# Two more channel tiles of each depthwise convolution without tap matmuls: products on ScalarE, sums on GpSimd

## The chip, the cores and the metric

The kernel runs on one core of one Trainium2 chip. The metric is the device time of one execution in microseconds (us). The kernel before was timed three times, with a median of 2589.94 us (2589.64 to 2590.89). One further execution was profiled; it took 2588.89 us. All points of time below are microseconds from the start of that execution's span.

## The reference, cut to what matters

The program is a four-layer encoder on 512 tokens and 1024 channels in float32. Layers 0 and 3 use the convolution module as their token mixer, so it runs twice. Only that module is touched:

```python
def dwconv(x, w, b):                      # w is (31, 1024): each channel has its own 31 taps
    k, c = w.shape
    y = lax.conv_general_dilated(x, w[:, None, :], window_strides=(1,),
        padding=[(k // 2, k // 2)], dimension_numbers=('NWC', 'WIO', 'NWC'), feature_group_count=c)
    return y + b

def conv_module(h, w_in, b_in, dw_w, dw_b, ln_g, ln_b, w_out):
    a, gt = jnp.split(h @ w_in + b_in, 2, axis=-1)
    u = a * jax.nn.sigmoid(gt)
    u = dwconv(u, dw_w, dw_b)
    u = layernorm(u, ln_g, ln_b)          # over all 1024 channels of a token
    return jax.nn.silu(u) @ w_out
```

The layer norm needs all channels of a token, so nothing behind it starts before the last channel tile of the convolution is complete.

## The kernel before, in words

The 1024 channels are eight tiles of 128. `conv` works through them in the order `CORDER`. For each tile m, `front(m)` multiplies the input by two weight tiles (value and gate). Each product is three matmuls of 128x512 per 128 input channels (`mm3`, L157 to L159), because a float32 operand is split into a high and a low part: ScalarE casts the high part (L152), VectorE subtracts to get the low part (L153). Then VectorE and ScalarE scale, gate and write the result.

Seven tiles go through TensorE. Their gated result `u` (L407) is spread by four small DMAs on GpSimd's queue (`xf`, L412) and split into `X` (L167, L168). `taps(m, X, half)` loads a prepared matrix of taps per 32 channels (`wraw`, SyncE's queue), splits it into `W` (ScalarE's cast L167, VectorE's subtraction L168) and runs nine pairs of matmuls: L445 (256 columns) and L448 (128 columns). A tile has four such matrices, thus 36 pairs. Two additions on VectorE (L457, L460) bring the sums with the bias into `y`.

One tile, number 6, is made by `direct` on VectorE alone: its gated result is `ud` (L403), and 31 instructions (L421, L423) each multiply a shifted view by one tap and add it to `yd`. Four transposes on TensorE (L428) and a copy on ScalarE (L429) bring it into `y`.

`bn_stats` (L465) reads finished column groups of `y`. Behind the last tap matmul stand 23 matmuls without use (`NWARM`, L470) that fill TensorE's wait for the statistics. Then `norm` starts with transposes (L510), and the output product follows.

The program is built with a scheduler that sets each engine's order from its own model of the times. Within an engine the order is fixed, and an instruction that waits holds everything behind it on that engine. `issue_after` pins an instruction behind another one.

Of the kernel before, what the change touches and what calls it, by code (L numbers as in the profile page):

```python
# [17 lines left out]
P = 128  # L18
# [14 lines left out]
_n = 0  # L33
for _name, _w in (
    ("n1g", 32), ("n2g", 32), ("cbin", 32), ("clg", 16), ("clb", 16), ("qg", 1), ("kg", 1), ("gng", 16), ("logd", 8),
    ("fdw", 4 * 44 * FC), ("fdb", 4 * 44), ("cwd", 2 * CW), ("cbd", 2),
):
    COLS[_name] = _n
    _n += _w
# [20 lines left out]
NRAW = 2  # L60
HPO = 100000
NQZ = 2
BNG = ((0, 8, 8), (8, 14, 12), (14, 15, 15), (15, 16, 16))
NWARM = 23
CD = 6
CORDER = (CD, 0, 1, 2, 3, 4, 5, 7)
CTAPS = (0, 3, 5, 5, 5, 5, 5, 3, 0, 0)


@with_exitstack  # L70
def tile_trunk(
# [17 lines left out]
    def nm(s):  # L89
        uid[0] += 1  # L90
        return f"{s}{uid[0]}"
# [11 lines left out]
    def bank(which):  # L103
        return cur[which].tile([P, T], F32, tag="ps", name=nm("ps"))
# [246 lines left out]

    def conv(j, after):
        with ExitStack() as st:
            stage_pools(st, 9, 4, 4)
            cp = st.enter_context(tc.tile_pool(name=nm("cv"), bufs=1, reuse_waits=RW))
            y = cp.tile([P, SH, D], F32, tag="y", name=nm("y"))
            bias = cp.tile([P, D], F32, tag="bias", name=nm("bias"))
            early = kind == "conv" and j == 0 and bool(first)
            if not early:
                nc.scalar.dma_start(bias, cdb[j])  # L360
            bst = cp.tile([P, SH, len(BNG), 6], F32, tag="bst", name=nm("bst"))
            with ExitStack() as s2:
                up = s2.enter_context(tc.tile_pool(name=nm("cvu"), bufs=1, reuse_waits=RW))
                dp = s2.enter_context(tc.tile_pool(name=nm("cvd"), bufs=2, reuse_waits=RW))
                us = [up.tile([P, SH, QL], F32, tag=f"u{i}", name=nm("u")) for i in range(2)]
                ud = up.tile([P, T + CW - 1], F32, tag="ud", name=nm("ud"))
                yd = up.tile([P, T], F32, tag="yd", name=nm("yd"))
                nc.vector.memset(ud[:, :CW // 2], 0.0)
                nc.vector.memset(ud[:, T + CW // 2:], 0.0)
                for u in us:  # L370
                    nc.vector.memset(u[:, :, :4], 0.0)
                    nc.vector.memset(u[:, :, QL - 4:], 0.0)
# [2 lines left out]
                    nc.vector.tensor_copy(ap, sqacc[:, :1])  # L375

                def front(m):
                    where = psb if early and m == CD else psa
                    pa, pg = bank(where), bank(where)
                    ws = state.pop("first", None) if m == CD else None  # L380
                    if ws:
                        for k in range(KD):
                            s = slice(k * P, (k + 1) * P)
                            for ps, (wh, wl) in zip((pa, pg), ws):
                                mm3(ps, wh[:, s], wl[:, s], xhi[k], xlo[k], k == 0, k == KD - 1)
                        after_squares(bias[:, :1])
                        nc.scalar.dma_start(bias, cdb[j])
                        stats1()
                        stats2()
                    else:  # L390
                        for (ps, c) in ((pg, m + 8), (pa, m)):
                            wh, wl = load_w(cw_in[j, c], D)
                            for k in range(KD):
                                s = slice(k * P, (k + 1) * P)
                                mm3(ps, wh[:, s], wl[:, s], xhi[k], xlo[k], k == 0, k == KD - 1)
                            if m == CD:
                                stats2() if c == m else stats1()
                    ta, tg = t512(), t512()
                    nc.vector.tensor_tensor(tg, pg, rstd_bc, MUL)
                    nc.scalar.activation(tg, tg, AF.Sigmoid, bias=pc("cbin", j * 16 + 8 + m))  # L400
                    nc.vector.tensor_tensor(ta, pa, rstd_bc, MUL)
                    if m == CD:
                        nc.vector.scalar_tensor_tensor(  # L403
                            ud[:, CW // 2:CW // 2 + T], ta, pc("cbin", j * 16 + m), tg, ADD, MUL)
                        return None
                    u = us[m % 2]
                    state["u"] = nc.vector.scalar_tensor_tensor(  # L407
                        u[:, :, 4:4 + P], ta.rearrange("p (q s) -> p s q", s=SH),
                        pc("cbin", j * 16 + m), tg.rearrange("p (q s) -> p s q", s=SH), ADD, MUL)
                    xf = dp.tile([P, 4, QL], F32, tag="xf", name=nm("xf"))  # L410
                    for b in range(4):
                        nc.gpsimd.dma_start(xf[:, b, :], u[32 * b:32 * b + 32])  # L412
                    X = dp.tile([P, 4, 2, QL], F32R, tag="X", name=nm("X"), bufs=3)
                    split(xf, X[:, :, 0, :], X[:, :, 1, :])
                    return X

                def direct(k0, k1):
                    for k in range(k0, k1):
                        w = pc("cwd", j * CW + k)
                        if k == 0:  # L420
                            nc.vector.tensor_scalar(yd, ud[:, :T], w, pc("cbd", j), MUL, ADD)  # L421
                        else:
                            nc.vector.scalar_tensor_tensor(yd, ud[:, k:k + T], w, yd, MUL, ADD)  # L423
                    if k0 < k1 == CW:
                        ps = bank(psb)
                        yr = yd.rearrange("p (q r) -> p r q", r=SH)
                        for r in range(SH):
                            nc.tensor.transpose(ps[:, r * P:(r + 1) * P], yr[:, r], ident)  # L428
                        nc.scalar.copy(y[:, :, CD * P:(CD + 1) * P],  # L429
                                       ps.rearrange("p (r c) -> p r c", r=SH))  # L430

                def taps(m, X, half):
                    ps = bank(psb)
                    for i in range(2):
                        b = half * 2 + i
                        raw = dp.tile([P, NA, P], F32, tag="wraw", name=nm("wraw"), bufs=5)
                        if early and m * 4 + b < 5:
# [3 lines left out]
                        with tc.issue_after(state["u"].ins) if early and m * 4 + b < 5 else ExitStack():  # L441
                            split(raw, W[:, :, 0, :], W[:, :, 1, :])
                        o = ps[:, i * 256:(i + 1) * 256]
                        for a in range(NA):
                            nc.tensor.matmul(o, X[:, b, 0, a:a + P],  # L445
                                             W[:, a].rearrange("p h n -> p (h n)"),
                                             start=a == 0, stop=False)
                            mm = nc.tensor.matmul(o[:, :P], X[:, b, 1, a:a + P], W[:, a, 0, :],  # L448
                                                  start=False, stop=a == NA - 1)
# [3 lines left out]
                    bb = bias[:, c0:c0 + 64].rearrange("p (b c) -> p b c", b=2)  # L453
# [8 lines left out]
                    for n, (a0, a1, at) in enumerate(BNG):  # L462
                        if c1 == at:
                            for r in range(SH):
                                nc.vector.bn_stats(bst[:, r, n, :], y[:, r, a0 * 64:a1 * 64])  # L465
                    if c1 == 16:
                        wp = bank(psa)
                        with tc.issue_after(mm.ins):
# [2 lines left out]
                        with tc.issue_after(state["cast"].ins):  # L471
                            nc.scalar.activation(sm(1), zero, AF.Silu)

                fr, done = {}, 0
                for n in range(10):
                    if n < 8:
                        fr[n] = front(CORDER[n])
                    direct(done, done + CTAPS[n])
                    done += CTAPS[n]
                    if n >= 3:  # L480
                        taps(CORDER[n - 2], fr[n - 2], 1)
                    if 2 <= n <= 8:
                        taps(CORDER[n - 1], fr[n - 1], 0)
            mv = sm(8)
            for r in range(SH):
# [528 lines left out]
    kind, l = seq[0]  # L1014
    first = []
    if kind == "conv":
        for c in (CD, CD + 8):
# [48 lines left out]
def _layout(inp):  # L1066
# [31 lines left out]
    cd = slice(CD * P, (CD + 1) * P)  # L1098
    put("cwd", f["conv_dw_w"][:, :, cd].transpose(2, 0, 1).reshape(P, -1))
    put("cbd", f["conv_dw_b"][:, cd].T)  # L1100
# [74 lines left out]
```

## Time and profile before

| What | us |
|---|---|
| Median of three runs | 2589.94 |
| Profiled execution, its own time | 2588.89 |
| Its span | 2586.8 |
| TensorE busy | 2575.8 |
| VectorE busy | 1664.1 |
| ScalarE busy | 1041.4 |
| GpSimd busy | 229.9 |
| Tap matmuls of the first convolution, from and to | 55.8 to 156.5 |
| First transpose of `norm`, first and second convolution | 162.0 and 2161.7 |

A group row of the profile names line, engine, operation, output and inputs, shape and count, then busy time and mean duration of one in ns, then the idle time of the engine ahead of the group with what ended it. A row of the timeline gives start, duration, engine, line and instruction, and how many equal ones it merges. Matmuls overlap in the timeline, so the pace of a series is read from the distance of two starts, not from a duration. TensorE's granted clock is 1.0 throughout.

### The profile page before, as it was taken

Reading aid. Unit: us, or ns where it says so; the run is one execution under the profiler, and the core shown is the slowest. Engines: PE = TensorE matmul, PEld = TensorE weight load, DVE = VectorE, ACT = ScalarE, POOL = GpSimd, SP = SyncE. Lnnn points to the kernel's source line nnn. Section 1 sums busy time; section 2 is a strip of 40 time slices with the busy share of each in tenths; the row PEclk is TensorE's granted clock in tenths of the full one; section 3 lists DMA queues with packets and bytes.
Section 4 is the critical chain, followed back from the end, with each engine's and each line's share of the span. In section 5 each row is a group of like instructions: output and inputs, shape, how many; then the busy total and the mean of one; then the engine's idle time right before and its main releaser. Section 6 shows DMA issues by size and latency. Waiting matters only on the chain.

```text
span 2586.8 us, 32299 instructions
## 1 busy us (share of the span) xinstructions
PE 2575.8 (100%) x12750; PEld 2138.5 (83%) x12750; DVE 1664.1 (64%) x2688; ACT 1041.4 (40%) x1423; POOL 229.9 (9%) x245
## 2 busy tenths in 40 slices
PE   9999999999999999999999999999999999999999
PEld 7988888889998888888888888888888888788888
DVE  7976777438878777624656566677733877677732
ACT  5454444335555444323333333444422445444421
POOL 0103000003421100000000000100000111100000
PEclk9999999999999999999999999999999999999999
DMA  6724222333332322333222221222233662222232
GB/s 226 230 74 153 98 90 96 90 100 111 97 91 70 99 98 92 92 97 110 74 87 68 88 75 61 101 91 98 89 92 97 215 195 70 93 90 98 89 109 80
DMA packets 78376, 269.86 MB, mean 104 GB/s; under 512 B 9824, under 2 KB 12768, under 8 KB 78224
## 3 DMA queue, kind: packets, MB, share of 16 engines
q1 hardware_dynamic: 73152, 254.49, 30.3%
q0 software_dynamic: 3776, 10.58, 1.5%
q10 hardware_dynamic: 1296, 2.72, 0.3%
q8 instruction: 100, 1.64, 0.3%
q14 instruction: 52, 0.43, 0.1%
HBM read 258.35 MB, written 5.63 MB: 102 GB/s over the span
## 4 chain that ended last, share of the span: by engine, by line
PE 98%; DVE 1%; DMA 0%; ACT 0%; issue 0%; SPq 0%; DVEq 0%
PE ps L157 27%; PE ps L158 27%; PE ps L159 27%; PE ps L445 3%; PE ps L163 3%; PE ps L164 3%; PE ps L162 3%; PE ps L448 1%; PE ps L314 1%; PE ps L315 1%; PE ps L319 1%; PE ps L692 1%; PE ps L470 0%; DMA x<-in_xT 0%; PE ps L510 0%; PE ps L918 0%
## 5 line engine op out<-in xcount | busy, mean ns | idle before, releaser
L152 ACT CAST wh<-wr 128x1024 fp32r<-128x1024 f32 (+1 forms) x410 | 423.0, 1033 | 1077.9 <-PE ps L158 766.3
L158 PE MATMUL ps<-xl,wh 128*128 128x512 f32 x1856 | 735.8, 397 | 0.1
L157 PE MATMUL ps<-xh,wh 128*128 128x512 f32 x1856 | 733.1, 396 | 0.2 <-ACT wh L152 0.2
L159 PE MATMUL ps<-xh,wl 128*128 128x512 f32 x1856 | 731.5, 394 | 0.1
L153 DVE TENSOR_TENSOR wl<-wr,wh 128x1024 fp32r<-128x1024 f32 (+1 forms) x407 | 494.0, 1214 | 327.8 <-ACT wh L152 325.5
L157 PEld LDWEIGHTS ps<-xh,wh 128*128 128x128 f32 x1856 | 348.6, 188 | 86.7 <-ACT wh L152 0.9
L159 PEld LDWEIGHTS ps<-xh,wl 128*128 128x128 f32 x1856 | 348.3, 188 | 84.1 <-DVE wl L153 0.5
L158 PEld LDWEIGHTS ps<-xl,wh 128*128 128x128 f32 x1856 | 348.5, 188 | 82.2 <-DVE xl L216 0.5
L157 PE MATMUL ps<-hh,wh 128*128 128x512 f32 (+1 forms) x726 | 281.8, 388 | 0.5 <-DVE x L344 0.5
L159 PE MATMUL ps<-hh,wl 128*128 128x512 f32 (+1 forms) x726 | 281.8, 388 | 0.0
L158 PE MATMUL ps<-hl,wh 128*128 128x512 f32 (+1 forms) x726 | 281.8, 388 | 0.0
L280 DVE TENSOR_TENSOR t<-ps,rstd_bc 128x512 f32<-128x512 f32 x176 | 121.0, 691 | 158.5 <-PE ps L159 158.5
L234 POOL TENSOR_TENSOR sqacc<-t,sqacc 128x512 f32<-128x512 f32 x49 | 74.5, 1520 | 1262.3 <-ACT t L229 1261.8
L157 PEld LDWEIGHTS ps<-hh,wh 128*128 128x128 f32 x726 | 136.4, 188 | 31.7 <-DVE x L344 0.7
L159 PEld LDWEIGHTS ps<-hh,wl 128*128 128x128 f32 x726 | 136.4, 188 | 30.9
L158 PEld LDWEIGHTS ps<-hl,wh 128*128 128x128 f32 x726 | 136.4, 188 | 30.8
L163 PE MATMUL ps<-wl,xh 128*128 128x256 f32 (+1 forms) x512 | 159.2, 312 | 0.5 <-DVE wl L153 0.5
L164 PE MATMUL ps<-wh,xl 128*128 128x256 f32 (+1 forms) x512 | 159.1, 312 | 0.0
L162 PE MATMUL ps<-wh,xh 128*128 128x256 f32 (+1 forms) x512 | 158.5, 312 | 0.0
L283 ACT ACTIVATE t<-t,par 128x512 f32<-128x512 f32 x176 | 142.5, 814 | 6.7 <-DVE t L280 6.6
L287 DVE SCALAR_TENSOR_TENSOR t<-t,par,t 128x511 f32<-128x511 f32 x176 | 132.2, 751 | 5.6
L285 DVE SCALAR_TENSOR_TENSOR t<-t,par,t 128x511 f32<-128x511 f32 x176 | 131.1, 746 | 0.0
(244 smaller groups left out, 3445.0 us busy)
## 6 DMA issues: line engine op xcount, KB each, us to landing
wr<-in_f_up SPq DMA_DIRECT2D x176, 512.0 KB, 3.3
wraw<-in_cdw SPq DMA_DIRECT2D x56, 576.0 KB, 4.5
wr<-in_f_down SPq DMA_DIRECT2D x64, 448.0 KB, 3.3
wr<-in_f_down SPq DMA_DIRECT2D x32, 512.0 KB, 3.5
wr<-in_cw_in SPq DMA_DIRECT2D x30, 512.0 KB, 4.0
wr<-in_nat_qkv SPq DMA_DIRECT2D x24, 512.0 KB, 3.3
wr<-in_cw_out SPq DMA_DIRECT2D x16, 512.0 KB, 3.6
wr<-in_ret_qk SPq DMA_DIRECT2D x16, 512.0 KB, 3.2
```

The source lines that it names most:

```text
L152: nc.scalar.copy(hi[:, :n], raw[:, :n])
L153: eng.tensor_tensor(lo[:, :n], raw[:, :n], hi[:, :n].bitcast(F32), SUB)
L157: nc.tensor.matmul(o, wh, ah, start=first, stop=False)
L158: nc.tensor.matmul(o, wh, al, start=False, stop=False)
L159: nc.tensor.matmul(o, wl, ah, start=False, stop=last)
L162: nc.tensor.matmul(o, ah, wh, start=first, stop=False)
L163: nc.tensor.matmul(o, ah, wl, start=False, stop=False)
L164: nc.tensor.matmul(o, al, wh, start=False, stop=last)
L280: nc.vector.tensor_tensor(u, ps, rstd_bc, MUL)
L283: nc.scalar.activation(a, u, AF.Identity, bias=pc("fdb", l * 44 + c), scale=pt[:, w + 1:w + 2])
L285: nc.vector.scalar_tensor_tensor(a[:, 1:], u[:, :T - 1], pt[:, w:w + 1], a[:, 1:], MUL, ADD)
L287: nc.vector.scalar_tensor_tensor(a[:, :T - 1], u[:, 1:], pt[:, w + 2:w + 3], a[:, :T - 1], MUL, ADD)
```

## The change: three tiles without tap matmuls

Tiles 1, 6 and 0 now come first and go around the tap matmuls (`CDIR`). Tile 0 gets all 31 taps on VectorE, as tile 6 did before. Tiles 1 and 6 get four taps on VectorE (`CVEC`); each of the other 27 becomes a product on ScalarE into a buffer `pr` (two buffers) and a sum into `yd` on GpSimd. `gather` transposes a finished tile on TensorE, pinned behind a tap matmul, and takes its statistics. `CSTEP` and `CDONE` say behind which front the steps are written down. Five tiles keep their tap matmuls. The temporaries go from nine to seven and the buffers of `wraw` from five to four, since the new tiles need room.

```diff
-BNG = ((0, 8, 8), (8, 14, 12), (14, 15, 15), (15, 16, 16))
+BNG = ((0, 8, ("d", 2)), (8, 12, 12), (12, 14, ("d", 1)), (14, 15, 15), (15, 16, 16))
-CD = 6
-CORDER = (CD, 0, 1, 2, 3, 4, 5, 7)
-CTAPS = (0, 3, 5, 5, 5, 5, 5, 3, 0, 0)
+CORDER = (1, 6, 0, 2, 3, 4, 5, 7)
+CDIR = (1, 6, 0)
+CVEC = (4, 4, 31)
+CSTEP = ((0, 0, 0, 31), (1, 1, 0, 31), (2, 2, 0, 3), (3, 2, 3, 10),
+         (4, 2, 10, 17), (5, 2, 17, 24), (6, 2, 24, 31))
+CDONE = {6: (0,), 7: (2,), 8: (1,)}
...
-            stage_pools(st, 9, 4, 4)
+            stage_pools(st, 7, 4, 4)
...
-                def direct(k0, k1):
+                def direct(i, k0, k1):
+                    ud, yd = uds[i], yds[i]
                     for k in range(k0, k1):
-                        w = pc("cwd", j * CW + k)
+                        w = pc("cwd", (j * 3 + i) * CW + k)
                         if k == 0:
-                            nc.vector.tensor_scalar(yd, ud[:, :T], w, pc("cbd", j), MUL, ADD)
+                            nc.vector.tensor_scalar(yd, ud[:, :T], w, pc("cbd", j * 3 + i), MUL, ADD)
+                        elif k < CVEC[i]:
+                            nc.vector.scalar_tensor_tensor(yd, ud[:, k:k + T], w, yd, MUL, ADD)
                         else:
-                            nc.vector.scalar_tensor_tensor(yd, ud[:, k:k + T], w, yd, MUL, ADD)
-                    if k0 < k1 == CW:
-                        ps = bank(psb)
-                        yr = yd.rearrange("p (q r) -> p r q", r=SH)
+                            pr = up.tile([P, T], F32, tag="pr", name=nm("pr"), bufs=2)
+                            nc.scalar.activation(pr, ud[:, k:k + T], AF.Copy, scale=w)
+                            nc.gpsimd.tensor_tensor(yd, pr, yd, ADD)
+
+                def gather(i):
+                    ps = bank(psb)
+                    yr = yds[i].rearrange("p (q r) -> p r q", r=SH)
+                    with tc.issue_after(state["tap"].ins):
                         for r in range(SH):
                             nc.tensor.transpose(ps[:, r * P:(r + 1) * P], yr[:, r], ident)
...
+                    stats(("d", i))
...
-                        raw = dp.tile([P, NA, P], F32, tag="wraw", name=nm("wraw"), bufs=5)
+                        raw = dp.tile([P, NA, P], F32, tag="wraw", name=nm("wraw"), bufs=4)
...
-                fr, done = {}, 0
+                fr, nd = {}, len(CDIR)
                 for n in range(10):
                     if n < 8:
                         fr[n] = front(CORDER[n])
-                    direct(done, done + CTAPS[n])
-                    done += CTAPS[n]
-                    if n >= 3:
+                    for (at, i, k0, k1) in CSTEP:
+                        if at == n:
+                            direct(i, k0, k1)
+                    if n - 2 >= nd:
                         taps(CORDER[n - 2], fr[n - 2], 1)
-                    if 2 <= n <= 8:
+                    for i in CDONE.get(n, ()):
+                        gather(i)
+                    if nd <= n - 1 < 8:
                         taps(CORDER[n - 1], fr[n - 1], 0)
```

The built order shows the change on the queues that the prediction speaks of. First GpSimd in the second convolution (`xf<-u` are the spreading DMAs, L412 before and L417 now; L433 is the new sum). Before:

```order
L234 TENSOR_TENSOR sqacc<-t_16858,sqacc 128x512
L412 DMA xf_17067<-u_16886 128x1x136 x4
L412 DMA xf_17146<-u_16887 128x1x136 x4
L412 DMA xf_17277<-u_16886 128x1x136 x4
L412 DMA xf_17458<-u_16887 128x1x136 x4
L412 DMA xf_17639<-u_16886 128x1x136 x4
L412 DMA xf_17820<-u_16887 128x1x136 x4
```

Now, from the thirteenth sum on:

```order
L433 TENSOR_TENSOR yd_16869<-pr_17025,yd_16869 128x512
L433 TENSOR_TENSOR yd_16869<-pr_17028,yd_16869 128x512
L417 DMA xf_17362<-u_16864 128x1x136 x4
L433 TENSOR_TENSOR yd_16869<-pr_17031,yd_16869 128x512
L433 TENSOR_TENSOR yd_16869<-pr_17034,yd_16869 128x512
L433 TENSOR_TENSOR yd_16869<-pr_17037,yd_16869 128x512
L433 TENSOR_TENSOR yd_16869<-pr_17040,yd_16869 128x512
L433 TENSOR_TENSOR yd_16869<-pr_17043,yd_16869 128x512
L417 DMA xf_17445<-u_16865 128x1x136 x4
```

GpSimd had nothing but 28 DMAs in a convolution. It now has 54 sums, 27 of one tile and then 27 of the next, with 20 DMAs between them.

Second TensorE near the end of the first convolution's taps, at the transposes of the last direct tile (`yd`). Before, where tile 6 was gathered (L428) ahead of the second half of tile 4's taps:

```order
L159 MATMUL ps_1266<-xh_92,wl_1300 128x512
L428 MATMUL ps_1345<-ident,yd_223 128x128 x4
L445 MATMUL ps_1351<-W_1354,X_973 128x256
L448 MATMUL ps_1351<-W_1354,X_973 128x128
L445 MATMUL ps_1351<-W_1354,X_973 128x256
```

Now, where tile 6 is gathered (L440) ahead of the taps of the last tile, 7 (L463 and L466 are the tap pair):

```order
L463 MATMUL ps_1419<-W_1445,X_1117 128x256
L466 MATMUL ps_1419<-W_1445,X_1117 128x128
L440 MATMUL ps_1473<-ident,yd_226 128x128 x4
L463 MATMUL ps_1483<-W_1486,X_1306 128x256
L466 MATMUL ps_1483<-W_1486,X_1306 128x128
```

The tile that GpSimd finishes last is now gathered ahead of the 36 tap pairs of tile 7 and of the matmuls without use. Until it is complete, TensorE's queue stands there.

Third ScalarE in the first convolution, where the new products (`pr<-ud`, L432) stand among the casts of weights. Before:

```order
L429 COPY y_211<-ps_1345 128x4x128
L167 CAST W_1427<-wraw_1425 128x9x128
L167 CAST W_1454<-wraw_1452 128x9x128
L167 CAST W_1477<-wraw_1475 128x9x128
L167 CAST X_1339<-xf_1334 128x4x136
```

Now:

```order
L171 CAST W_1486<-wraw_1484 128x9x128
L432 ACTIVATE pr_518<-ud_223,par 128x512
L171 CAST W_1509<-wraw_1507 128x9x128
L171 CAST X_1306<-xf_1301 128x4x136
L432 ACTIVATE pr_521<-ud_223,par 128x512
L432 ACTIVATE pr_524<-ud_223,par 128x512
L171 CAST W_1540<-wraw_1538 128x9x128
L432 ACTIVATE pr_527<-ud_223,par 128x512
```

A product waits for the sum that frees its buffer, and the casts that TensorE's taps need stand behind it.

More of the change, by code (lines that the diff above doesn't have):

```diff
@@ L353, in conv @@
         with ExitStack() as st:
[L354 removed]
+            stage_pools(st, 7, 4, 4)
             cp = st.enter_context(tc.tile_pool(name=nm("cv"), bufs=1, reuse_waits=RW))
             y = cp.tile([P, SH, D], F32, tag="y", name=nm("y"))
[L357 removed]
+            bias = cp.tile([P, D - CB], F32, tag="bias", name=nm("bias"))
             early = kind == "conv" and j == 0 and bool(first)
             if not early:
[L360 removed]
+                nc.scalar.dma_start(bias, cdb[j][:, CB:])
             bst = cp.tile([P, SH, len(BNG), 6], F32, tag="bst", name=nm("bst"))
@@ L365, in conv @@
                 us = [up.tile([P, SH, QL], F32, tag=f"u{i}", name=nm("u")) for i in range(2)]
[L366 to L369, printed above, removed]
+                uds = [up.tile([P, T + CW - 1], F32, tag=f"ud{i}", name=nm("ud")) for i in range(3)]
+                yds = [up.tile([P, T], F32, tag=f"yd{i}", name=nm("yd")) for i in range(3)]
+                for ud in uds:
+                    nc.vector.memset(ud[:, :CW // 2], 0.0)
+                    nc.vector.memset(ud[:, T + CW // 2:], 0.0)
                 for u in us:
@@ L377, in front @@
                 def front(m):
-                    where = psb if early and m == CD else psa
+                    where = psb if early and m == CORDER[0] else psa
                     pa, pg = bank(where), bank(where)
-                    ws = state.pop("first", None) if m == CD else None
+                    ws = state.pop("first", None) if m == CORDER[0] else None
                     if ws:
@@ L386, in front @@
                         after_squares(bias[:, :1])
-                        nc.scalar.dma_start(bias, cdb[j])
+                        nc.scalar.dma_start(bias, cdb[j][:, CB:])
                         stats1()
@@ L435, in taps @@
                         b = half * 2 + i
-                        raw = dp.tile([P, NA, P], F32, tag="wraw", name=nm("wraw"), bufs=5)
-                        if early and m * 4 + b < 5:
+                        raw = dp.tile([P, NA, P], F32, tag="wraw", name=nm("wraw"), bufs=4)
+                        if early and CORDER.index(m) * 4 + b < 4 * len(CDIR) + 5:
                             after_squares(raw[:, 0, :1])
@@ L440, in taps @@
                         W = dp.tile([P, NA, 2, P], F32R, tag="W", name=nm("W"), bufs=3)
-                        with tc.issue_after(state["u"].ins) if early and m * 4 + b < 5 else ExitStack():
-                            split(raw, W[:, :, 0, :], W[:, :, 1, :])
+                        split(raw, W[:, :, 0, :], W[:, :, 1, :])
                         o = ps[:, i * 256:(i + 1) * 256]
@@ L461, in taps @@
                     c1 = m * 2 + half + 1
[L462 to L465, printed above, removed]
+                    state["tap"] = mm
+                    stats(c1)
                     if c1 == 16:
@@ L1016, in tile_trunk @@
     if kind == "conv":
-        for c in (CD, CD + 8):
+        for c in (CORDER[0], CORDER[0] + 8):
             first.append((wraw.tile([P, D], F32, tag="wr", name=nm("wr")),
```

26 lines of the change are left out of this document (16 added, 10 removed).

## The prediction

> **What bounds the kernel now.** First the page's busy times and its chain of waits, then the timeline of TensorE in the stage that changes.
>
> ```profile
> PE 2575.8 (100%) x12750; PEld 2138.5 (83%) x12750; DVE 1664.1 (64%) x2688; ACT 1041.4 (40%) x1423; POOL 229.9 (9%) x245
> PE 98%; DVE 1%; DMA 0%; ACT 0%; issue 0%; SPq 0%; DVEq 0%
> ```
>
> TensorE is the chain for 98% of the span, so a matmul that goes is a gain as long as nothing else becomes late. Whether anything does is read from the two stretches of tap matmuls, 55.0 to 156.4 and 2037.0 to 2156.4 (columns: length, then busy us and instructions of each engine, granted clock, DMA share, GB/s):
>
> ```profile
> core 0: us, PE busy (x) PEld busy (x) DVE busy (x) ACT busy (x) POOL busy (x), PEclk, DMA share, GB/s
> 55.00:156.40 101.40, 101.40 (x693) 93.00 (x692) 89.78 (x118) 47.83 (x49) 10.80 (x20) 1.00 0.58 185
> 2037.00:2156.40 119.40, 119.40 (x770) 107.56 (x769) 97.87 (x128) 51.96 (x55) 13.12 (x25) 1.00 0.53 168
> ```
>
> The reader is to see two things. TensorE is never idle and has its full clock, so it does set the end. But VectorE is busy for 89.8 of 101.4 us and 97.9 of 119.4 us: here, unlike in the rest of the program, the second engine is close behind. GpSimd is nearly idle, and it is where the change puts its work.
>
> **The gain on TensorE.** Nine pairs of taps run between the two matmuls of `mm3` below; then the gather of the direct tile and the end of the stage:
>
> ```profile
> 102.14 0.28 PE L445 MATMUL ps<-W,X 128*128 128x256 f32 x1
> 104.17 0.44 PE L158 MATMUL ps<-xl,wh 128*128 128x512 f32 x1
> 135.37 0.63 PE L428 MATMUL ps<-ident,yd 128*128 128x128 f32 x4
> 135.75 0.37 PE L445 MATMUL ps<-W,X 128*128 128x256 f32 x1
> 156.55 5.46 PE L470 MATMUL ps<-xh 128*128 128x512 f32 x23
> 162.04 0.30 PE L510 MATMUL ps<-ident,yn 128*128 128x128 f32 x1
> 2156.16 5.46 PE L470 MATMUL ps<-xh 128*128 128x512 f32 x23
> 2161.66 0.92 PE L510 MATMUL ps<-ident,yn 128*128 128x128 f32 x5
> ```
>
> Nine pairs take 104.17 - 102.14 = 2.03 us, a tile's 36 pairs 8.1 us. Two tiles go per convolution (16.2 us) and two gathers of 0.38 us come: 15.5 us less for TensorE per convolution, 31 us in all. Alone on the path this gives 2588.9 - 31 = 2558 us, the most that the change can bring.
>
> **What ScalarE gets.** 54 products per convolution. No row has one; the nearest 128x512 rows of ScalarE with a scale or bias are these:
>
> ```profile
> L213 ACT ACTIVATE xh<-x,png 128x512 fp32r<-128x512 f32 x64 | 50.7, 798 | 33.3 <-DVE x L523 16.4 <-DVE x L256 12.9 <-DVE x L251 3.6
> L400 ACT ACTIVATE t<-t,par 128x512 f32<-128x512 f32 x16 | 11.5, 723 | 1.9 <-DVE t L399 1.8
> L167 ACT CAST W<-wraw 128x1152 fp32r<-128x1152 f32 x25 | 29.0, 1159 | 34.7 <-PE ps L448 32.5 <-issue 1.3 <-ACT t L400 1.0
> ```
>
> 54 at 0.72 to 0.80 us are 39 to 43 us; eight casts of `W` at 1.16 us (the last row, of the first stretch) go. Net some 32 us on an engine with 47.8 of 101.4 us busy: 80 us, which fits. So ScalarE's time costs nothing by itself; its order may (a rival below).
>
> **What GpSimd gets.** 54 sums per convolution, each reading two tiles from SBUF and writing one, 128x512. The same form exists: `sqacc` (L234). Its rows alone, and then where VectorE splits weights (L153) beside it:
>
> ```profile
> L234 POOL TENSOR_TENSOR sqacc<-t,sqacc 128x512 f32<-128x512 f32 x49 | 74.5, 1520 | 1262.3 <-ACT t L229 1261.8
> 841.40 1.30 POOL L234 TENSOR_TENSOR sqacc<-t,sqacc 128x512 f32<-128x512 f32 x1
> 842.77 1.29 POOL L234 TENSOR_TENSOR sqacc<-t,sqacc 128x512 f32<-128x512 f32 x1
> 846.59 1.29 DVE L153 TENSOR_TENSOR wl<-wr,wh 128x1024 fp32r<-128x1024 f32 x1 [5.40 <-ACT wh L152]
> 846.87 2.16 POOL L234 TENSOR_TENSOR sqacc<-t,sqacc 128x512 f32<-128x512 f32 x1
> 847.80 2.31 DVE L153 TENSOR_TENSOR wl<-wr,wh 128x1024 fp32r<-128x1024 f32 x1
> 849.11 2.15 POOL L234 TENSOR_TENSOR sqacc<-t,sqacc 128x512 f32<-128x512 f32 x1
> 188.29 1.31 POOL L234 TENSOR_TENSOR sqacc<-t,sqacc 128x512 f32<-128x512 f32 x1 [48.33 <-ACT t L229]
> 188.35 1.80 DVE L216 SCALAR_TENSOR_TENSOR xl<-x,png,xh 128x512 fp32r<-128x512 f32 x1
> 1230.64 1.30 POOL L831 TENSOR_TENSOR t<-t,t 128x512 f32<-128x512 f32 x1
> 1231.02 0.68 DVE L827 TENSOR_TENSOR t<-ps,sn 128x512 f32<-128x512 f32 x1
> ```
>
> Alone, sums that follow each other start every 1.37 us. Beside VectorE's splits they start every 2.24 us, and VectorE's split takes 2.31 us where its mean is 1.22 in the groups below. So the two take turns. This concerns VectorE instructions with both tensors in SBUF; the one that reads `ps` (PSUM) runs at its 0.68 us beside a sum. How long a sum shuts VectorE out: the split is 2.31 - 1.22 = 1.09 us longer; the L216 instruction, 1.80 us against the 0.75 us of the same operation on `yd` below, is 1.05 us longer and began 0.06 us behind the sum. I take 1.10 us.
>
> The Trainium skill has a rule for this ("SBUF — State Buffer", section "Who interferes with whom"): a VectorE instruction with two SBUF inputs and a GpSimd instruction that reads SBUF use one shared port, and the later one is blocked until the first has finished. The trace agrees on who blocks whom, but frees the port after about 1.10 of a sum's 1.29 us. By the page's full length the sum below would be 54 x 0.19 = 10 us higher per convolution, 2658 us by estimate.
>
> So I count the turns. VectorE's instructions with two SBUF inputs in both stretches:
>
> ```profile
> L168 DVE TENSOR_TENSOR W<-wraw,W 128x1152 fp32r<-128x1152 f32 x26 | 35.0, 1352 | 2.0 <-ACT W L167 2.0
> L423 DVE SCALAR_TENSOR_TENSOR yd<-ud,par,yd 128x512 f32<-128x512 f32 x24 | 17.9, 746 | 0.1
> L153 DVE TENSOR_TENSOR wl<-wr,wh 128x1024 fp32r<-128x1024 f32 x9 | 10.9, 1221 | 1.6 <-ACT wh L152 1.6
> L407 DVE SCALAR_TENSOR_TENSOR u<-t,par,t 128x512 f32<-128x512 f32 x5 | 5.7, 1146 | 0.1
> L168 DVE TENSOR_TENSOR X<-xf,X 128x544 fp32r<-128x544 f32 x6 | 4.3, 718 | 0.0
> L168 DVE TENSOR_TENSOR W<-wraw,W 128x1152 fp32r<-128x1152 f32 x25 | 33.9, 1357 | 3.2 <-ACT W L167 3.2
> L423 DVE SCALAR_TENSOR_TENSOR yd<-ud,par,yd 128x512 f32<-128x512 f32 x27 | 20.2, 750 | 0.2
> L153 DVE TENSOR_TENSOR wl<-wr,wh 128x1024 fp32r<-128x1024 f32 x12 | 14.6, 1220 | 0.3 <-ACT wh L152 0.3
> ```
>
> In the changed order, behind the fourth VectorE tap of the first direct tile, the first convolution has 17 `W`, 31 `yd`, 9 `wl`, 5 `u` and 5 `X`: 17 x 1.352 + 31 x 0.746 + 9 x 1.221 + 5 x 1.146 + 5 x 0.718 = 66.4 us. The second has 17, 33, 12, 5, 5 and one `ud` (0.75): 72.6 us. With 54 x 1.10 = 59.4 us of sums the port is taken for 125.8 and 132.0 us. VectorE instructions overlap by about 0.09 us (the split at 847.80 starts before the one ahead ends, 846.59 + 1.29), which for 67 and 73 of them takes off 6.0 and 6.6 us; on the other side the port rests whenever both wait. I take half: 122.8 and 128.7 us.
>
> Where it starts: the scale `rstd_bc` must be there.
>
> ```profile
> 35.44 0.59 ACT L247 COPY rstd_bc<-ps 128x512 f32<-128x512 f32 x1 [2.60 <-PE ps L193]
> 2027.64 0.59 ACT L247 COPY rstd_bc<-ps 128x512 f32<-128x512 f32 x1 [2.19 <-PE ps L193]
> L412 POOL DMA_DIRECT2D xf<-u x56 | 30.5, 566 | 236.5 <-DVE u L407 169.6 <-issue 36.4 <-ACT W L167 30.5
> ```
>
> From there to the fourth tap VectorE has some 21 instructions in the first convolution (seven scalings, three gates, two splits, nine taps), about 16 us, and a weight still on its way: first sum near 55 (51 to 57). In the second convolution a dozen, about 9 us: near 2037.
>
> The last sum then ends at 55 + 122.8 = 177.8 and 2037 + 128.7 = 2165.7. TensorE's queue stands at the gather of that tile. Behind it come 0.4 us of transposes, tile 7's 8.1 us of taps and 5.5 us of matmuls without use before `norm`: 14.0 us, giving 191.8 and 2179.7, against 162.0 and 2161.7 now. **That is +29.8 and +18.0, together +48 us.** TensorE's saving is inside it: its taps would be ready near 141 and 2141 and wait. Other stalls of TensorE ahead of that gather cost nothing while it is early by so much.
>
> Bounds from GpSimd's own queue: 20 DMAs at 0.57 us (11.4 us) and 54 sums at 1.37 or 2.24 us are 85 or 132 us. By the first, `norm` starts at 55 + 85.4 + 14.0 = 154.4 (-7.6) in the first convolution, and in the second TensorE sets the end (-15.5): 2566 us. By the second it starts at 55 + 132.4 + 14.0 = 201.4 (+39.4) and 2037 + 132.4 + 14.0 = 2183.4 (+21.7): 2650 us. My 122.8 and 128.7 us correspond to 2.06 and 2.17 us per sum, near the upper row, because VectorE nearly always has such an instruction ready. With p for a sum's price both convolutions together change by 108 p - 181 us, so the zero lies at 1.68 us per sum.
>
> Edits that I cost at nothing: fewer temporaries, four buffers for `wraw` and 24 fewer loads on SyncE's queue in all, covered by TensorE's long wait; if the first lacks cover, a front waits one scaling (0.7 us) each. Tile 0's 31 VectorE taps replace those of tile 6. The DMAs that now stand behind sums on GpSimd delay `X` by up to a sum or two (2 to 4 us), under the same cover. All stages outside the two convolutions keep their order.
>
> The profiled execution is 1.05 us under the median of the runs; with +48 on the median I predict 2638 us.
>
> **Rivals.** *Sums fit in beside VectorE (faster).* If GpSimd keeps its 1.37 us, because the turns are rare, the time is the 2566 us above. For it speaks that most of the 49 `sqacc` rows are nearer to 1.3 than to 2.2 (mean 1.52). Against it: those ran where VectorE had gaps, and here VectorE is busy for 89%. It decides below 1.68 us. Chance 0.08.
>
> *ScalarE's order starves the sums.* ScalarE waits 34.7 us for TensorE to free `W` in front of the casts of the first stretch (the L167 row). With 17 casts left that is some 23 us, and the products behind such a cast wait too, with two buffers ahead. If half of it lets GpSimd rest, each convolution is 12 us longer: 2662 us. Against it: TensorE is early, so its buffers come free sooner relative to GpSimd. Chance 0.17.
>
> *A draw*, a price between 1.6 and 1.75 us per sum, 2581 to 2597 us: chance 0.06. That the change does not do what it says is excluded: TensorE has 288 tap matmuls fewer and 16 transposes more.
>
> **How the numbers follow.** The forecast, turns at the port with ends between 2600 and 2655 us, has 0.69. A measurement of this kernel tells some 0.2% (5 us) from no change. Slower holds the forecast, the ScalarE rival and most of the draw: 0.89. Faster: 0.09. Same: 0.02. The range leaves out the faster rival and little above: 2600 to 2664 us, which includes the page's rule, the upper row and the ScalarE rival.
>
> **What would show it.** Right: sums (L433) that take 2 us or more in most cases, VectorE's `yd`, `W` and `wl` well above 0.75, 1.36 and 1.22 us, a wait of TensorE of some 25 to 35 us in front of the last gather (L440) in the first convolution, and less in the second, where waits for `W` share it. Wrong: sums near 1.3 us and TensorE without gaps (the faster rival), or long rests of GpSimd between sums that ended by ScalarE's products (the other one). If the order ahead of the gather matters more than I think, waits for `W` ahead of tap matmuls would be the larger part.

## The result, and the profile after

The kernel after the change takes 2649.4 us (median; 2648.6 to 2649.8), the kernel before beside it 2590.2 us (2589.6 to 2590.9). The ratio is 1.023, with a 95% interval of 1.0217 to 1.0243: 59 us slower. Forecast were 2638 us and a range of 2600 to 2664. The profiled execution took 2649.3 us, with a span of 2646.8 us. Two executions of kernels below had TensorE slow from its first matmul on, ahead of all changed code, and are left out of every comparison: 8946 us for the kernel without the sums and 3602 us for the last kernel.

First the same two lines of the page as before the change, now for the kernel after:

```profile
PE 2571.0 (97%) x12478; PEld 2126.8 (80%) x12478; DVE 1720.4 (65%) x2684; ACT 1092.6 (41%) x1515; POOL 406.3 (15%) x337
PE 90%; DVE 6%; issue 2%; POOL 1%; ACT 1%; DMA 0%; SPq 0%; DVEq 0%; POOLq 0%; ACTq 0%
```

TensorE executes 272 matmuls fewer, but it is busy for only 4.8 us less, and its share of the chain falls from 98% to 90%. VectorE has taken 6% and GpSimd 1%. The two stages with tap matmuls, by stretches (columns as before: length, busy us and instructions of PE, PEld, DVE, ACT and POOL, granted clock, DMA share, GB/s):

```profile
55.00:188.00 133.00, 92.73 (x530) 82.56 (x529) 112.25 (x103) 70.27 (x91) 100.57 (x74) 0.85 0.33 104
2050.00:2192.00 142.00, 125.44 (x635) 106.77 (x634) 128.48 (x127) 76.53 (x98) 94.42 (x69) 0.92 0.41 138
```

TensorE, without a gap here before, now stands for 40 of 133 us, and its granted clock is 0.85. What it waits for in the first convolution, 55 to 200 us (columns: us in total, times, longest):

```profile
PE ps L440 <- POOL yd L433: 27.9, 2, 22.9
PE ps L463 <- DVE W L172: 12.3, 6, 6.8
```

The larger wait is the one at the gather of the tile that GpSimd finishes last, the smaller one the matrices that VectorE prepares. TensorE's timeline shows the end of that wait, the taps behind it and the start of `norm`, then the same places in the second convolution (columns: start, us, instruction, idle time ahead):

```profile
180.90 1.12 PE L440 MATMUL ps<-ident,yd 128*128 128x128 f32 x4 [22.93 <-POOL yd L433]
181.68 0.56 PE L463 MATMUL ps<-W,X 128*128 128x256 f32 x1
182.14 0.52 PE L463 MATMUL ps<-W,X 128*128 128x256 f32 x1
...
185.07 0.33 PE L463 MATMUL ps<-W,X 128*128 128x256 f32 x1
...
185.29 0.33 PE L463 MATMUL ps<-W,X 128*128 128x256 f32 x1
...
197.12 1.52 PE L529 MATMUL ps<-ident,yn 128*128 128x128 f32 x8
2203.82 1.13 PE L440 MATMUL ps<-ident,yd 128*128 128x128 f32 x4 [7.60 <-POOL yd L433]
...
2220.59 1.52 PE L529 MATMUL ps<-ident,yn 128*128 128x128 f32 x8
```

`norm` starts 197.1 - 162.0 = 35.1 us later in the first convolution. In the second it starts 2220.6 - 2161.7 = 58.9 us later, of which 35.1 us come from the first, so the second adds 23.8 us. The whole loss of 59 us arises in these two stages.

VectorE's instructions between 55 and 190 us (groups by shape; busy us, then mean ns of one), and the new sums in the whole program (duration in ns, smallest, median and largest; then what GpSimd waited for ahead of them):

```profile
L429 DVE SCALAR_TENSOR_TENSOR yd<-ud,par,yd 128x512 f32<-128x512 f32 x30 | 41.3, 1380 | 0.3
L172 DVE TENSOR_TENSOR W<-wraw,W 128x1152 fp32r<-128x1152 f32 x17 | 29.7, 1750 | 3.1 <-ACT W L171 3.1
L157 DVE TENSOR_TENSOR wl<-wr,wh 128x1024 fp32r<-128x1024 f32 x9 | 16.6, 1841 | 0.0
L412 DVE SCALAR_TENSOR_TENSOR u<-t,par,t 128x512 f32<-128x512 f32 x5 | 7.8, 1570 | 0.0
L172 DVE TENSOR_TENSOR X<-xf,X 128x544 fp32r<-128x544 f32 x5 | 6.4, 1289 | 0.0
L404 DVE TENSOR_TENSOR t<-ps,rstd_bc 128x512 f32<-128x512 f32 x4 | 2.7, 676 | 0.0
L433 POOL TENSOR_TENSOR yd<-pr,yd x108: 1261/1626/2455, 54.4 to 2201.5; 128x512 f32<-128x512 f32 x108
  ACT pr L432: 25.0, 15
```

The instructions with two inputs in SBUF have grown: `yd` from 746 to 1380 ns, `W` from 1352 to 1750, `wl` from 1221 to 1841. The one that reads `ps` in PSUM takes 676 ns, as before. The sums have a median of 1.63 us, where a sum alone took 1.3. GpSimd also rested 25 us, in 15 places, until a product was ready.

### The profile page after: what moved, and what is told of

Read it like the earlier page. It is cut to its first block, busy times and chain, and to the rows that moved or that the text cites. A ratio compares the mean times of both kernels' runs of the same rounds, so it can differ in the third digit from the quotient of the medians.

```text
span 2646.8 us, 31952 instructions
## 1 busy us (share of the span) xinstructions
PE 2571.0 (97%) x12478; PEld 2126.8 (80%) x12478; DVE 1720.4 (65%) x2684; ACT 1092.6 (41%) x1515; POOL 406.3 (15%) x337
## 4 chain that ended last, share of the span: by engine, by line
PE 90%; DVE 6%; issue 2%; POOL 1%; ACT 1%; DMA 0%; SPq 0%; DVEq 0%; POOLq 0%; ACTq 0%
PE ps L162 26%; PE ps L161 26%; PE ps L163 25%; PE ps L167 3%; PE ps L168 3%; PE ps L166 3%; DVE yd L429 2%; POOL yd L433 1%; PE ps L463 1%; DVE W L172 1%; DVE wl L157 1%; PE ps L318 1%; PE ps L319 1%; PE ps L323 1%; PE ps L711 1%
## 5 line engine op out<-in xcount | busy, mean ns | idle before, releaser
L157 DVE TENSOR_TENSOR wl<-wr,wh 128x1024 fp32r<-128x1024 f32 (+1 forms) x407 | 505.3, 1242 | 330.4 <-ACT wh L156 328.0
L433 POOL TENSOR_TENSOR yd<-pr,yd 128x512 f32<-128x512 f32 x108 | 185.0, 1713 | 108.8 <-DVE yd L429 77.6
L291 DVE SCALAR_TENSOR_TENSOR t<-t,par,t 128x511 f32<-128x511 f32 x176 | 132.0, 750 | 5.5
```

The costliest lines, as they stand in the source:

```text
L157: eng.tensor_tensor(lo[:, :n], raw[:, :n], hi[:, :n].bitcast(F32), SUB)
L291: nc.vector.scalar_tensor_tensor(a[:, :T - 1], u[:, 1:], pt[:, w + 2:w + 3], a[:, :T - 1], MUL, ADD)
L433: nc.gpsimd.tensor_tensor(yd, pr, yd, ADD)
```

## The experiments

The theory: a sum on GpSimd reads two tiles from SBUF and shuts VectorE's instructions with two SBUF inputs out, so both engines' work adds up on one resource, and the tile that ends last holds TensorE. The rivals: ScalarE's products starve the sums; the work on GpSimd is slow by itself, or its queue is; the place of the gather costs more than the sums do. The table has the times of all kernels but the last and the start of `norm` in both convolutions; the experiments in it are single executions (thirteen of the kernel before lay between 2588.4 and 2591.3 us).

| Kernel | us | `norm`, 1st | `norm`, 2nd |
|---|---|---|---|
| before | 2590.2 | 162.0 | 2161.7 |
| after | 2649.4 | 197.1 | 2220.6 |
| without sums | 2559.2 | 146.8 | 2131.2 |
| sums without products | 2651.7 | 199.2 | 2223.6 |
| GpSimd only writes | 2569.8 | 157.0 | 2141.4 |
| all taps on VectorE | 2609.7 | 179.3 | 2182.0 |
| less work on VectorE | 2616.1 | 182.6 | 2187.6 |
| last gather later | 2643.6 | 189.4 | 2213.0 |
| half the sums, two tiles | 2612.6 | 175.6 | 2184.6 |
| two tiles, all on VectorE | 2590.0 | 168.6 | 2162.1 |

**Without the sums.** The products still run; nothing adds them.

```diff
-                            nc.gpsimd.tensor_tensor(yd, pr, yd, ADD)
```

> The changed kernel without the 54 sums per convolution on GpSimd; the products on ScalarE stay and are read by nobody (tiles 1 and 6 hold their first four taps only). Theory (turns at SBUF): VectorE at its own speed, TensorE sets the end, 2555 to 2575 us, near the 2570 us that the kernel with memsets in place of the sums took. Rival (the order and the products delay the taps): above 2610 us.

Measured: 2559.2 us, against 2589.5 before. VectorE's groups, 55 to 160 us:

```profile
L429 DVE SCALAR_TENSOR_TENSOR yd<-ud,par,yd 128x512 f32<-128x512 f32 x30 | 22.3, 747 | 0.3
L157 DVE TENSOR_TENSOR wl<-wr,wh 128x1024 fp32r<-128x1024 f32 x9 | 11.0, 1219 | 0.2 <-ACT wh L156 0.2
```

All that the change brings TensorE, 15.2 us in the first convolution and 30.5 in both, is there as soon as the sums are gone, and VectorE's durations are those of before. The order of the fronts, the gathers, the 54 products per convolution and the longer VectorE share cost nothing that can be seen. The sums cost 90 us, of which TensorE's saving hides a third.

**The sums without the products.** GpSimd adds the shifted view itself, so it never waits for ScalarE; the tap weights are left out.

```diff
-                            pr = up.tile([P, T], F32, tag="pr", name=nm("pr"), bufs=2)
-                            nc.scalar.activation(pr, ud[:, k:k + T], AF.Copy, scale=w)
-                            nc.gpsimd.tensor_tensor(yd, pr, yd, ADD)
+                            nc.gpsimd.tensor_tensor(yd, ud[:, k:k + T], yd, ADD)
```

> The changed kernel without the products on ScalarE: each sum adds the shifted tile itself instead of its product with the tap, so the values are wrong, but GpSimd reads two tiles from SBUF as before and waits for no product. Theory (turns at SBUF): the same sums against the same VectorE work, 2640 to 2658 us. Rival (ScalarE's order with two product buffers starves the sums, 12 us per convolution): 2630 us or less.

Measured: 2651.7 us, no faster than with the products. The edit changes more than it was meant to, though: in the built order the sums of tiles 1 and 6 now alternate, where the kernel after makes 27 of the one and then 27 of the other. GpSimd's sums and TensorE's waits from 55 to 205 us, then four rows: a VectorE tap, the sums from 75.6 to 89.5 us beside it, TensorE's first gather, and VectorE's next instruction behind that gather:

```profile
L431 POOL TENSOR_TENSOR yd<-ud,yd x54: 1080/1282/2260, 54.8 to 164.5; 128x512 f32<-128x512 f32 x54
PE ps L438 <- POOL yd L431: 30.4, 1, 30.4
PE ps L461 <- DVE W L172: 14.3, 2, 13.6
75.50 14.58 DVE L429 SCALAR_TENSOR_TENSOR yd<-ud,par,yd 128x512 f32<-128x512 f32 x1
L431 POOL TENSOR_TENSOR yd<-ud,yd 128x512 f32<-128x512 f32 x12 | 13.9, 1220 | 0.0
163.28 1.13 PE L438 MATMUL ps<-ident,yd 128*128 128x128 f32 x4 [30.38 <-POOL yd L431]
169.06 1.36 DVE L172 TENSOR_TENSOR W<-wraw,W 128x1152 fp32r<-128x1152 f32 x1 [21.58 <-ACT W L171]
```

With products out of the way the last sum is done 15 us sooner (165.6 instead of 180.8), and `norm` still starts 2.1 us later. Two things cost what was gained. Sums that wait for nothing need not take turns with VectorE: beside twelve of them in a row a tap of 0.75 us took 14.58 us, and TensorE then waited 13.6 us for `W`. And the first gather, which has the 108 tap pairs of three tiles behind it, is released at 163.3 us, with two sums still to come; in the kernel after it is released at 130.6. VectorE is idle for 21.6 us meanwhile, because the casts that it needs wait behind that gather. So this run doesn't settle what ScalarE's order costs. It shows that sums which come sooner are no gain by themselves.

**GpSimd only writes.** Each sum is replaced by two instructions that fill `yd` with zeros, so GpSimd has a queue of similar length that reads nothing.

```diff
-                            nc.gpsimd.tensor_tensor(yd, pr, yd, ADD)
+                            for _ in range(2):
+                                nc.gpsimd.memset(yd, 0.0)
```

> The changed kernel with each sum on GpSimd replaced by two memsets of the same tile yd (tiles 1 and 6 are left without their convolution). GpSimd is busy for about 2 x 0.52 us per step, stands in the same queue with the same DMAs, and the gather still waits for its last step, but it reads nothing. Theory in its narrow form (it is the reading of SBUF that shuts VectorE out): VectorE's W and wl splits stay at 1.36 and 1.22 us, GpSimd ends near 55 + 11 + 54 x 1.2 = 131 us, TensorE sets the end: 2555 to 2580 us. Rival (any busy GpSimd shuts VectorE out, or GpSimd's long queue delays the tiles X): 54 x 1.04 = 56 us per convolution taken from VectorE, 2635 us or more, with splits above 1.5 us.

Measured: 2569.8 us. GpSimd's and VectorE's groups, 55 to 160 us:

```profile
L434 POOL MEMSET yd<- 128x512 f32 x108 | 51.6, 581 | 53.6 <-DVE yd L429 53.3
L429 DVE SCALAR_TENSOR_TENSOR yd<-ud,par,yd 128x512 f32<-128x512 f32 x30 | 22.3, 745 | 0.3
L157 DVE TENSOR_TENSOR wl<-wr,wh 128x1024 fp32r<-128x1024 f32 x9 | 11.0, 1221 | 6.0 <-ACT wh L156 6.0
```

Two fills are 1.16 us, not far from a lone sum's 1.3, but VectorE keeps its 745 and 1221 ns: GpSimd's reading shuts it out, not its being busy. The fills don't wait for products either, so this run speaks of VectorE's durations and not of those waits. The Trainium skill says so of write-only instructions ("SBUF — State Buffer", section "Who interferes with whom"); the trace agrees. Nor is GpSimd's queue as such too slow: TensorE waits 5.4 us for it, at the first gather, and this kernel is 20 us faster than the one before.

**All 31 taps of all three tiles on VectorE.** GpSimd has no sums, ScalarE no products.

```diff
-CVEC = (4, 4, 31)
+CVEC = (31, 31, 31)
```

> The changed kernel with all 31 taps of all three tiles on VectorE, no products and no sums on GpSimd; nothing is left out. Theory (turns): a tap costs VectorE 0.66 us itself, but 1.1 us when GpSimd adds it, so taking GpSimd's help away makes it faster: VectorE's work after the start is 66 + 21 + 54 x 0.66 = 123 us if nothing overlaps, less 0.09 us of overlap each, near 110, where the port was taken for 126: 2605 to 2625 us. Rival (VectorE is full and GpSimd relieves it): 54 x 0.66 = 36 us more per convolution, above 2700 us.

Measured: 2609.7 us, 40 us faster than with GpSimd's help. VectorE's group and TensorE's wait in the first convolution:

```profile
L429 DVE SCALAR_TENSOR_TENSOR yd<-ud,par,yd 128x512 f32<-128x512 f32 x84 | 57.7, 747 | 0.0
PE ps L440 <- DVE yd L429: 28.1, 1, 28.1
```

A tap takes 57.7 / 84 = 0.69 us of VectorE when it makes it alone. The 40 us over 108 taps are 0.37 us more for each tap that is handed to GpSimd. Help that goes through the same resource is a loss here.

**Less work on VectorE.** Tile 0 gets only its first four taps; the other 27 are left out. The sums stay.

```diff
-                    for k in range(k0, k1):
+                    for k in range(k0, min(k1, 4) if i == 2 else k1):
```

> The changed kernel without taps 4 to 30 of tile 0 on VectorE (27 instructions per convolution left out, so tile 0 is incomplete); all products and sums stay. Theory (turns): the port is taken for 27 x 0.66 = 18 us less per convolution, and each sum waits less, so 2610 to 2625 us with sums that get shorter than the 1.71 us mean of the changed kernel. Rival (GpSimd's chain runs at its own pace, set by its queue and the products): 2640 to 2650 us, sums as long as before.

Measured: 2616.1 us, as expected: 33 us come back although no sum was touched. One detail was a miss. The sums did not get shorter, as the first row (whole program) shows; behind it what GpSimd waited for, VectorE's group, 55 to 160 us, and GpSimd's timeline:

```profile
L433 POOL TENSOR_TENSOR yd<-pr,yd x108: 1260/1628/3178, 54.3 to 2169.4; 128x512 f32<-128x512 f32 x108
  ACT pr L432: 7.9, 7
L172 DVE TENSOR_TENSOR W<-wraw,W 128x1152 fp32r<-128x1152 f32 x16 | 30.9, 1943 | 4.2 <-ACT W L171 4.2
110.77 11.74 POOL L433 TENSOR_TENSOR yd<-pr,yd 128x512 f32<-128x512 f32 x7
144.06 21.52 POOL L433 TENSOR_TENSOR yd<-pr,yd 128x512 f32<-128x512 f32 x15 [2.23 <-ACT pr L432]
```

The durations are a poor gauge: the splits that VectorE still has take the same turns, and the seven sums from 110.77 on take 1.68 us each. The last fifteen follow at 1.43 us; VectorE has only an `X` and two `W` left by then. The gain lies in when the last sum ends, 165.6 instead of 180.8. GpSimd's rests for products fall from 25.0 to 7.9 us with it, though no product was touched, so most of them came with VectorE's work.

**The last gather later.** Tile 6 is gathered one place further back, behind tile 7's taps.

```diff
-CDONE = {6: (0,), 7: (2,), 8: (1,)}
+CDONE = {6: (0,), 7: (2,), 9: (1,)}
```

> The changed kernel with the last gather (tile 6) written down behind the taps of tile 7 instead of in front of them; nothing is left out. Theory (in the first convolution the last sum sets the end, and what stands behind the gather on TensorE is added to it): the 36 pairs of tile 7, 9.9 us with the slow clock behind the wait, move into the wait: 7 to 10 us less in the first convolution, less in the second where W is late as well, 2632 to 2643 us. Rival (the late W set the end, the gather merely shows it): within 2 us of 2649 us.

Measured: 2643.6 us, a gain of 5.8 us, a little less than expected. TensorE's waits for the statistics in the whole program, and its clock behind the second of them (the number behind ACT's and POOL's is the granted clock):

```profile
PE ps L529 <- DVE yn L527: 10.3, 2, 5.2
2213.00:2215.00 2.00, 1.90 (x8) 1.46 (x8) 1.10 (x5) 1.17 (x3) 0.00 (x0) 0.50 0.01 4
```

The first convolution gains 197.1 - 189.4 = 7.7 us. The second takes 2213.0 - 189.4 = 2023.6 us from one `norm` to the next, where the kernel after takes 2023.5: there TensorE waits for `W` as well (10.9 us, against 7.6 us for the sums, in the kernel after from 2050 to 2230), and another place of the gather doesn't help that. At the second `norm` the gain is thus 7.6 us; some of it is lost behind it, where TensorE has waited 5.1 us for the statistics and goes on at half its clock. The order is a tenth of the loss.

**Half the sums, and none.** Two direct tiles instead of three: tile 6 with 4 taps on VectorE and 27 by product and sum, tile 0 on VectorE (`(4, 31)`); then both on VectorE (`(31, 31)`).

```diff
-CORDER = (1, 6, 0, 2, 3, 4, 5, 7)
-CDIR = (1, 6, 0)
-CVEC = (4, 4, 31)
+CORDER = (6, 0, 1, 2, 3, 4, 5, 7)
+CDIR = (6, 0)
+CVEC = (4, 31)
...
-CDONE = {6: (0,), 7: (2,), 8: (1,)}
+CDONE = {8: (0,), 7: (1,)}
```

> Two direct tiles instead of three, in both convolutions: tile 0 with 31 taps on VectorE, tile 6 with four on VectorE and 27 products and sums; six tiles keep their tap matmuls; nothing is left out. Theory (turns): TensorE saves half, 7.7 us per convolution, and 27 sums shut VectorE out for 30 us in a stretch in which it was busy for 90 of 101 us: 5 to 13 us longer per convolution, 2600 to 2616 us. Rival (only the length of GpSimd's chain counts, and with half of it the chain ends early): 2575 us.

> The same kernel as the one with half the sums, but with all 31 taps of tile 6 on VectorE too: two direct tiles, no products and no sums on GpSimd; nothing is left out. Theory (turns): a tap on VectorE costs it 0.66 us and a sum on GpSimd costs it 1.1 us, so this one is the faster of the two, by some 27 x 0.44 = 12 us per convolution at most, and stands near the kernel before: 2580 to 2595 us. Rival (GpSimd relieves VectorE): slower than with half the sums, above 2610 us.

Measured: 2612.6 us with 27 sums per convolution, 2590.0 us with none. TensorE's waits in the first convolution for the one and in the whole program for the other:

```profile
PE ps L462 <- DVE W L171: 13.0, 4, 4.9
```

```profile
PE ps L439 <- DVE yd L428: 11.0, 1, 11.0
```

With half the sums no gather waits; TensorE waits for matrices from a VectorE that is shut out. Without them VectorE is just too slow for a second tile in the first convolution (`norm` 6.6 us later than before) and fast enough in the second (2162.1 - 168.6 = 1993.5 us from one to the other, before 1999.6: 6.1 us less). The two cancel. Over 54 taps, 2612.6 - 2590.0 is 0.42 us per tap that goes to GpSimd, close to the 0.37 of three tiles.

**The second tile in the second convolution alone.** The first convolution has its tiles and steps as before the change (its gather stands one step later, and the buffers are those of the changed kernel); the second has tiles 6 and 0 on VectorE. The tables are chosen per convolution.

```diff
+        CDIR, CORDER, CVEC, CB, CSTEP, CDONE, BNG = (
+            ((6,), (6, 0, 1, 2, 3, 4, 5, 7), (31,), 0, ...),
+            ((6, 0), (6, 0, 1, 2, 3, 4, 5, 7), (31, 31), P, ...),
+        )[j]
```

> All taps of the direct tiles on VectorE, no sums on GpSimd; the first convolution with one direct tile (6) as before the change, the second with two (6 and 0) as in the kernel with two VectorE tiles; nothing is left out. From that kernel's trace: the second convolution gave 6.1 us (1993.5 against 1999.6 us between the two first norm transposes) and the first lost 6.6 us in a wait for VectorE. If both parts are independent: 2590 - 6 = 2582 to 2587 us, faster than both kernels. Rival (the second convolution gained only because the first ended in another state of the pools): 2590 us.

Measured: 2583.4 us (median of nine) against 2589.5, a ratio of 0.9976 with an interval of 0.9966 to 0.9986. That is 6 us less than the kernel before: small, but outside the noise, and what the second convolution alone had been expected to give. No trace shows where these 6 us arise.

## Why the prediction was right, and where its sizes were off

- **TensorE saves 31 us.** Shown: without the sums the time is 2559.2 us, where 2558 was worked out.
- **Sums lengthen VectorE's two-input instructions.** Shown from both sides: taking the sums away or making them write-only gives VectorE its durations back, and taking VectorE's taps away lets the sums end sooner. That the two take turns one by one is not the rule throughout: in the kernel without products twelve sums went ahead of one tap. The start of the first sum, 54.4 us and 2073.0 - 35.1 = 2037.9, was forecast as 55 and 2037.
- **The time of the turns.** The last sum ends 180.8 and 2203.8 - 35.1 = 2168.7, forecast 177.8 and 2165.7: 3 us too early each. That this is so close is in part luck. The windows from the first sum to the last, in the first convolution cut where VectorE has nothing left to do (columns as in the stretches above):

```profile
54.40:165.40 111.00, 86.23 (x486) 75.92 (x485) 110.66 (x98) 60.33 (x78) 86.59 (x63) 0.90 0.39 125
165.40:180.85 15.45, 0.00 (x0) 0.00 (x0) 0.00 (x0) 7.30 (x11) 14.58 (x12) 0.50 0.00 0
2073.00:2203.80 130.80, 106.28 (x562) 91.72 (x560) 123.08 (x108) 72.17 (x93) 105.35 (x74) 0.89 0.37 122
```

  With VectorE's groups in these windows the prediction's sum can be made again, term by term (the lone durations are those of the kernel before):

  | us | forecast, 1st | measured, 1st | forecast, 2nd | measured, 2nd |
  |---|---|---|---|---|
  | VectorE's two-input instructions, at lone durations | 66.4 | 64.3 | 72.6 | 71.2 |
  | what the sums add to them | 59.4 | 36.1 | 59.4 | 38.4 |
  | sums alone, VectorE done | 0 | 15.4 | 0 | 0 |
  | VectorE's other instructions | 0 | 16.6 | 0 | 19.9 |
  | VectorE idle | 0 | 0.3 | 0 | 7.7 |
  | overlap of VectorE's instructions | -3.0 | -6.3 | -3.3 | -6.4 |
  | sum | 122.8 | 126.4 | 128.7 | 130.8 |

  The 1.10 us per sum was too high: beside VectorE a sum cost it 36.1 / 42 = 0.86 and 38.4 / 54 = 0.71 us, and some twelve ran alone at the end. VectorE's instructions off the port were put at nothing, and its idle time too. The overlap took place in full, not by half. These errors nearly cancel, to 3.6 and 2.1 us.
- **The tail from gather to `norm`.** Forecast 14.0 us, measured 197.1 - 180.9 = 16.2 and 2220.6 - 2203.8 = 16.8. This term was added up from rows at full clock, and the clock was not full. These are the windows of TensorE's clock around its wait (from 158.0 on it has no matmul; it resumes at 180.9; the number behind POOL's is the granted clock):

```profile
160.00:161.00 1.00, 0.00 (x0) 0.00 (x0) 1.00 (x1) 0.28 (x1) 0.92 (x2) 1.00 0.00 0
161.00:162.00 1.00, 0.00 (x0) 0.00 (x0) 1.00 (x3) 0.44 (x1) 1.00 (x1) 0.54 0.00 0
184.00:185.00 1.00, 1.00 (x6) 1.00 (x6) 0.00 (x0) 0.00 (x0) 0.00 (x0) 0.51 0.00 0
185.00:186.00 1.00, 1.00 (x11) 1.00 (x10) 0.00 (x0) 0.51 (x1) 0.00 (x0) 1.00 0.00 0
```

  Three us into the wait the clock falls to half, and it returns some 4 us behind its end. In between, pairs of taps start every 0.43 us (181.68 to 182.14 and on), behind it every 0.22 (185.07 to 185.29). Eight slow pairs are 1.6 us, and the slower transposes make up most of the rest of the 2.2 us. In the second convolution the slow clock lasts a little longer (rows in the last section).
- **The sum.** 3.0 + 2.2 us in the first convolution and 3.0 + 2.8 in the second are 11 us: with 48 forecast, 59 measured.
- **The signs.** VectorE's durations rose as forecast. Two other signs did not come: most sums are shorter than 2 us (median 1.63), because a good part of the time from one to the next is rest, and TensorE's wait at the last gather of the first convolution is 22.9 us, where 25 to 35 were named.
- **The rivals.** That the sums fit in beside VectorE fell: with the 11 us of DMAs taken off, as in the prediction's own count, a sum takes (126.4 - 11.1) / 54 = 2.13 us from one to the next, and (130.8 - 11.0) / 54 = 2.22 in the second convolution, above the 1.68 of the zero. ScalarE's order was a real wait, 25 us in 15 places, as much as the 12 us per convolution of this rival. What it costs by itself was not separated, because the kernel without products also changed the order of the sums. As a rough bound, the rests are 25 us beside the 90 that the sums cost. Its share is probably smaller: 17 of the 25 us go when only VectorE's taps are taken out, and in the first convolution VectorE works on through GpSimd's rests until 165.4 us.
- **The place of the gather** was not among the rivals. It is worth 5.8 us in all, less than the sums by far.

## What to carry to other kernels

Price work that is handed to a helper by what it takes from the engine that it shares a resource with: here a tap cost VectorE 0.69 us when it made it itself, and the kernel was some 0.4 us slower for each tap that GpSimd "helped" with. Where two engines share a resource, forecast when both are done, count also what each does off it, and don't read much into the mean duration of either or into which of them the slow engine waits for last. And test the change by stage: the same second tile lost 6.6 us in one convolution and won 6.1 in the other, and only the half that won is worth keeping.

## What the runs showed of the hardware that had not been expected

**A row of sums can shut VectorE out for longer than one of them.** Beside twelve sums on GpSimd that followed each other in 13.9 us, a single VectorE tap took 14.58 us instead of 0.75 (the kernel without products).

**A wait of TensorE costs more than its length.** The clock rows above show 0.50 for about 4 us behind a wait of 22.9 us, some 2 us of lost time. Behind the wait of 7.6 us in the second convolution, which began at 2196.2 and ended at 2203.8 us, it is about 5 us and a little more loss (columns: length, PE, granted clock, DMA share, GB/s):

```profile
2198.00:2199.00 1.00, 0.00 (x0) 0.92 0.00 0
2208.00:2209.00 1.00, 1.00 (x7) 0.50 0.00 0
2209.00:2210.00 1.00, 1.00 (x11) 0.96 0.00 0
```

The Trainium skill ("TensorE: Matmul & The Clock Gate", section "Part 1: The HAM clock gate") gives about 3.4 us of idleness for the fall and about 3.4 us of work for the return. The trace agrees roughly, not exactly: the clock falls 3.1 and 2.6 us into these two waits and is back 4.1 and 5.3 us behind them.
